# Products in different row halves of the array issued in turn, and a tap table stored contiguously, in a two-layer RWKV-7 / S5 trunk

## Chip, core and metric

The kernel runs on one core of a Trainium2 chip. The core has TensorE (PE in the profile; its weight loads are PEld), VectorE (DVE), ScalarE (ACT), GpSimd (POOL), and SyncE (SP), whose queue issues all DMAs here. The metric is the device time of one execution in microseconds; lower is better. Matrix products write to PSUM; the kernel's four PSUM pools hold eight banks of 128 partitions x 512 float32.

## What is computed

A batch of one sequence, 1024 frames of 1024 channels, goes through two layers. Layer 0 mixes frames with RWKV-7 (16 heads of 64 channels, a 64x64 state per head); layer 1 with a diagonal complex state-space scan (64 groups of 16 channels with 64 states each). Each mixer is followed by a squared-ReLU MLP, and every sub-layer by a residual and a LayerNorm.

```python
def step(state, inp):                       # RWKV-7, per head
    r_t, w_t, k_t, v_t, a_t, b_t = inp
    sa = einsum('bhvk,bhk->bhv', state, a_t)
    state = state * w_t + sa[..., None] * b_t + v_t[..., None] * k_t
    return state, einsum('bhvk,bhk->bhv', state, r_t)
...
w_pre = w0 + tanh(xw @ w1) @ w2             # "rates": decay and in-context rate
a = sigmoid(a0 + (xa @ a1) @ a2)
...
s = abar * s + bbar @ u                     # S5, complex, per group
y = Re(c @ s) + d * u
x = layer_norm(alpha * x + f(x)); f = mixer or square(relu(x @ w1)) @ w2
```

## The kernel before

Channels lie on partitions and frames on the free axis, in two halves of 512 frames. The large products run as float32r triples: operand and weight are each split into a high and a low part (`split`, line 148/149), and `mm3` issues high x high, high x low and low x high. Weights are streamed as 256 KB blocks (`wload`: one DMA on SP, a cast on ACT, a subtraction on DVE). The other products are plain float32; the trace shows each of them as two weight loads and two matmuls, which are called **records** here (256 chunk products of line 596 are 512 records).

A product whose operands lie on 64 partitions uses one half of the array's rows; one with 64 weight columns uses one half of its columns. The trace shows this as rows*columns, for example 64*128.

The order of the work is that of a list scheduler: every instruction has a priority (the `rank` blocks), and the scheduler lays out each engine's queue when the kernel is built. On the chip every engine then runs its queue in that fixed order. The places that the change touches:

- **Rates** (`rates`, line 382, 16 calls in the projection stage). The second factors of decay and rate lie in the upper and lower 64 rows of one weight tile; six products of 64 rows x 512 frames go into two banks `pp[0]`, `pp[1]` of the three-bank pool `pd`.
- **Chunk matrices** (`amat`, line 580, for 8 units in the RWKV core). For each of two channel groups `j` and two chunk pairs `c2`, eight products of 64 rows (line 596) make four chunk matrices for head half `h` = 0 in one bank and four for `h` = 1 in another. Both are the tag "a" of pool `pa`, which has two banks; `elem` of the next unit uses the same two banks for its own small products. DVE masks each bank into `AT` (line 599). The masked matrices go into `invert` and into `chain`, the recurrence over chunks (pR, pX, pU, pO).
- **Tap table** (`s5_tables`, line 1038). For 8 blocks `f` of 128 channels the taps of the causal convolution within 8 frames are computed (line 1151), copied by ACT into the padded tile `kpad` with the group index innermost (line 1155), and stored by two DMAs for each `f` into `tT` (line 1159). The tables `tB` (input to state) and `tC` (state to output) are stored in the same loop.
- **Readout** (`s5`, from line 1235, once for each half of the frames). For four pairs `f2` of blocks, `tT` and `tC` are loaded into four buffers of the tag "tab". For each parity `par`, eight **tap products** (line 1250, all 128 rows, 64 columns, moving operand `tv` at a step of four elements) and sixteen **state products** (line 1255, the 64 rows that belong to `par`) are summed in one bank `py` of the two-bank pool `pc`. ACT copies each bank into `y1` (line 1257); eight transposes per block and a GELU follow, and the result goes out to `s_y`, which the GLU loads again. MLP products stand between the pairs `f2`.

## Time and profile before

| | |
|---|---|
| Median of three runs | 2736.43 us (2736.28 to 2744.62) |
| Profiled execution, its own time | 2746.6 us |
| Span of its trace | 2744.8 us |
| Mean granted TensorE clock | 0.961 |
| DVE / ACT / POOL busy | 66% / 42% / 23% |
| DMA | 345.90 MB, 126 GB/s on the mean |

Durations below come from the profiled execution, so sums are made against 2746.6 us and then carried over to the median. A matmul is pipelined: its duration is longer than the distance to the next one's start, so the cost of a run of matmuls is read from the start of its first to the start of what follows it. In a timeline row the first number is the start in us, the second the time from the first start to the last end, and x is the number of records. In a row of the groups, the numbers after the bar are busy us, mean ns of one, and idle us before them.

### The profile page before, as it was taken

To read this page: it belongs to the slowest core of one execution; us is meant where nothing else is said; L and a number is where in the kernel's file an instruction comes from. 1 tells how busy PE (TensorE), PEld (TensorE's weight loads), DVE (VectorE), ACT (ScalarE), POOL (GpSimd) and SP (SyncE) were. 2 spreads that over 40 slices of the span, in tenths; PEclk is the share of its full clock that TensorE was granted. 3 is DMA by queue.
4 is the path that set the end of the run, shared out by engine and by line. 5 is a ranking of instruction groups with operands and counts; after the bars stand their busy time and mean duration, and the time that the engine had idled before them with its cause. 6 is when DMAs were issued, how large, how long until landed. Compare 5 with 4: busy or idle time off the path is not lost.

```text
span 2744.8 us, 43807 instructions
## 1 busy us (share of the span) xinstructions
PE 2598.4 (95%) x16582; PEld 2089.9 (76%) x16582; DVE 1813.3 (66%) x3191; ACT 1154.8 (42%) x2038; POOL 630.6 (23%) x515
## 2 busy tenths in 40 slices
PE   7999979989899999989999999999999999999997
PEld 5778757678677777767876788778778887788886
DVE  7477677577786867997567553674855546755556
ACT  7455574544543333353532332434223324433334
POOL 3121542432442122342122000120220101210101
PEclk9989979999899999999999999999999999999998
DMA  4765455564223334545333533233343322333333
GB/s 146 235 214 175 151 164 156 178 203 142 81 86 88 93 92 148 141 129 163 100 112 127 174 95 100 81 96 112 103 164 110 96 96 81 119 96 96 96 96 100
DMA packets 215058, 345.90 MB, mean 126 GB/s; under 512 B 21184, under 2 KB 75584, under 8 KB 214848
## 3 DMA queue, kind: packets, MB, share of 16 engines
q1 hardware_dynamic: 214848, 343.10, 40.5%
q8 instruction: 131, 2.15, 0.3%
q14 instruction: 79, 0.65, 0.1%
HBM read 279.06 MB, written 63.96 MB: 125 GB/s over the span
## 4 chain that ended last, share of the span: by engine, by line
PE 44%; DVE 4%; issue 3%; DMA 1%; POOL 1%; ACT 1%; ACTq 0%; SPq 0%; DVEq 0%; POOLq 0%
PE d L188 39%; PE py L1250 1%; PE py L1255 1%; DVE wlo L149 1%; DMA wraw<-in_mw_dram 1%; PE pu L154 1%; PE pbu L1206 1%; POOL rl L975 1%; DVE hA L991 0%; DMA s_y<-yg 0%; DVE t L1218 0%; DVE hB L991 0%; ACT whi L148 0%; DVE sq L876 0%; PE pu L1195 0%
## 5 line engine op out<-in xcount | busy, mean ns | idle before, releaser
L148 ACT CAST whi<-wraw 128x512 fp32r<-128x512 f32 x668 | 413.5, 620 | 929.1 <-PE d L188 623.2
L149 DVE TENSOR_TENSOR wlo<-wraw,whi 128x512 fp32r<-128x512 f32 x668 | 500.6, 750 | 426.8 <-ACT whi L148 404.3
L188 PE MATMUL d<-qbuf,whi 128*128 128x512 f32 (+1 forms) x2112 | 657.0, 394 | 23.8 <-DVE hA L991 12.8
L188 PEld LDWEIGHTS d<-qbuf,whi 128*128 128x128 f32 x2112 | 391.8, 191 | 120.0 <-DVE hA L991 17.8
L188 PE MATMUL d<-qbuf,wlo 128*128 128x512 f32 (+1 forms) x1056 | 411.9, 392 | 10.7 <-DVE wlo L149 10.4
L975 POOL TENSOR_TENSOR rl<-rl 128x512 f32<-128x512 f32 x128 | 157.2, 1228 | 1094.5 <-ACT rl L974 1094.5
L188 PE MATMUL d<-oAh,whi 128*128 128x512 f32 (+1 forms) x960 | 390.9, 411 | 15.5 <-ACT ev L418 6.3
L188 PE MATMUL d<-oAl,whi 128*128 128x512 f32 (+1 forms) x960 | 387.5, 405 | 3.0 <-DVE oAl L149 2.8
L188 PE MATMUL d<-oAh,wlo 128*128 128x512 f32 (+1 forms) x960 | 386.5, 405 | 2.4 <-DVE wlo L149 2.3
L188 PE MATMUL d<-oBh,whi 128*128 128x512 f32 x704 | 279.2, 397 | 0.0
L188 PE MATMUL d<-oBh,wlo 128*128 128x512 f32 x704 | 278.7, 396 | 0.2 <-DVE wlo L149 0.2
L188 PE MATMUL d<-oBl,whi 128*128 128x512 f32 x704 | 277.1, 394 | 0.0
L188 PEld LDWEIGHTS d<-qbuf,wlo 128*128 128x128 f32 x1056 | 201.7, 191 | 56.5 <-DVE wlo L149 14.5
L188 PEld LDWEIGHTS d<-oAh,whi 128*128 128x128 f32 (+1 forms) x960 | 185.9, 194 | 62.2 <-ACT ev L418 8.4
L188 PEld LDWEIGHTS d<-oAh,wlo 128*128 128x128 f32 (+1 forms) x960 | 185.8, 194 | 44.4 <-DVE wlo L149 3.2
L188 PEld LDWEIGHTS d<-oAl,whi 128*128 128x128 f32 (+1 forms) x960 | 185.6, 194 | 43.1 <-DVE oAl L149 5.2
L991 DVE TENSOR_TENSOR hB<-hB,d 128x512 f32<-128x512 f32 (+1 forms) x256 | 165.0, 650 | 71.2 <-PE d L188 68.0
L991 DVE TENSOR_TENSOR hA<-hA,d 128x512 f32<-128x512 f32 x240 | 162.1, 682 | 64.4 <-PE d L188 62.1
L188 PEld LDWEIGHTS d<-oBh,wlo 128*128 128x128 f32 x704 | 132.9, 189 | 32.4 <-issue 2.0
L188 PEld LDWEIGHTS d<-oBl,whi 128*128 128x128 f32 x704 | 133.1, 189 | 29.9 <-issue 0.7
L188 PEld LDWEIGHTS d<-oBh,whi 128*128 128x128 f32 x704 | 133.1, 189 | 29.0 <-issue 1.2
L149 DVE TENSOR_TENSOR qbuf<-rl,qbuf 128x512 fp32r<-128x512 f32 x128 | 95.0, 742 | 73.5 <-ACT qbuf L148 73.5
(374 smaller groups left out, 3804.8 us busy)
## 6 DMA issues: line engine op xcount, KB each, us to landing
wraw<-in_mw_dram SPq DMA_DIRECT2D x520, 256.0 KB, 2.7
wraw<-in_glu_dram SPq DMA_DIRECT2D x64, 256.0 KB, 2.7
low<-wlo SPq DMA_DIRECT2D x52, 256.0 KB, 2.6
wlo<-low SPq DMA_DIRECT2D x52, 256.0 KB, 3.6
wraw<-in_wk_dram SPq DMA_DIRECT2D x32, 256.0 KB, 3.5
wraw<-in_wr_dram SPq DMA_DIRECT2D x32, 256.0 KB, 3.9
wraw<-in_wv_dram SPq DMA_DIRECT2D x32, 256.0 KB, 4.3
yl<-s_y SPq DMA_DIRECT2D x32, 256.0 KB, 3.1
```

Source lines behind the costliest of these rows:

```text
L148: S.copy(hi, src)
L149: (e or V).tensor_sub(lo, src, hi.bitcast(F32))
L154: PE.matmul(out, x, idt, start=True, stop=True)
L188: bulk.append((PE.matmul(p, w, x, **kw).ins, x.shape[-1]))
L975: G.tensor_mul(r, r, r)
L991: V.tensor_add(z, z, p)
L1206: PE.matmul(p[qs, g2, ri], tb[:, g2, ri, qs], u[:, 2 * g2 + par], start=True, stop=True)
L1250: PE.matmul(p[64 * j : 64 * j + 64, g2], ug[f][:, 2 * g2 + par], tv[:, par, g2], start=g2 == 0, stop=False, skip_group_check=True)
L1255: PE.matmul(p[64 * j : 64 * j + 64, g2], hb[qs, 4 * f + g2, ri, 0:NSC], tcm[qs, g2, ri], start=False, stop=ri == 1, skip_group_check=True)
```

## The change

Nothing that is computed changes. Four things do:

1. A helper `inorder` ties products together so that the scheduler keeps them in the order in which they are written. `mmb` now returns its matmul.
2. Rates and chunk matrices are written with the two row halves in turn (half 1 first), each into its own bank, and tied.
3. In the readout both parities' banks are opened together: sixteen tap products first, with the parities in turn, then 32 tied state products that go around (column half j, row half par). The two copies to `y1` stand behind all of them.
4. `kpad` is four times as large (four blocks `f`), with the taps of a group contiguous, and is stored after every fourth block by 2 x 8 DMAs of 16 partitions x 16 pieces of 128 elements. `tT` is laid out by partition; a load takes two pieces of 512 elements for each partition, and the tap products read a contiguous moving operand.

```diff
+TBF = 4
+    def inorder(prods):
+        for x, y in zip(prods, prods[1:]):
+            tc.add_manual_dep(y.ins, x.ins.name, ... NoSync ..., reason="order")
...
             for wi, xi in ((0, 0), (0, 1), (1, 0)):
-                for j in range(2):
+                for j in (1, 0):
                     js = slice(64 * j, 64 * j + 64)
-                    mmb(pp[j], w2[0][n % 4][wi][js], hx[xi][js], ...)
+                    prods.append(mmb(pp[j], w2[0][n % 4][wi][js], hx[xi][js], ...))
+            inorder(prods)
...
                     for i in range(2):
-                        for h in range(2):
+                        for h in (1, 0):
-                            PE.matmul(pp[h][:, cc, i], D.KB[j][hs, u], D.AR[j][hs, u], ...)
+                            prods.append(PE.matmul(pp[h][:, cc, i], D.KB[j][hs, u], D.AR[j][hs, u], ...))
+                inorder(prods)
...
-    tT = dr.tile([KT, 128, 2, 512], F32, name="tT")
+    tT = dr.tile([128, 2, KT, 4, 128], F32, name="tT")
-        kpad = pp.tile([128, 16, 16, 4], F32, name="kpad")
+        kpad = pp.tile([128, TBF, 4, 16, 16], F32, name="kpad")
...
-                S.copy(kpad[ps_, 8:].rearrange("p t c g -> p g (t c)"), p[ps_])
-            for par in range(2):
-                src = kpad[64 * par : 64 * par + 16, 1:9].rearrange("p t c g -> p (t c g)")
-                SP.dma_start(tv[par], bass.AP(src.tensor, src.offset, [src.ap[0], (64, SL), src.ap[1]]))
+                S.copy(kpad[ps_, f % TBF, :, 8:].rearrange("p g t c -> p g (t c)"), p[ps_])
+            if f % TBF == TBF - 1:
+                for par in range(2):
+                    for s in range(SL):
+                        SP.dma_start(
+                            tT[16 * s : 16 * s + 16, par, f - TBF + 1 : f + 1].rearrange("c f g n -> c (f g) n"),
+                            kpad[64 * par : 64 * par + 16, :, :, 1 + s : 9 + s].rearrange("c f g t e -> c (f g) (t e)"))
...
-            for par in range(2):
-                for g2 in range(4):
-                    for j, (f, tv, tcm) in enumerate(tabs):
-                        PE.matmul(p[64 * j : 64 * j + 64, g2], ug[f][:, 2 * g2 + par], tv[:, par, g2], ...)
-                for g2 in range(4):
-                    for ri in range(2):
-                        for j, (f, tv, tcm) in enumerate(tabs):
-                            PE.matmul(p[64 * j : 64 * j + 64, g2], hb[qs, 4 * f + g2, ri, 0:NSC], tcm[qs, g2, ri], ...)
-                S.copy(y1[:, :, :, par], p)
+            for g2 in range(4):
+                for par in range(2):
+                    for j, (f, tv, tcm) in enumerate(tabs):
+                        PE.matmul(pp[par][64 * j : 64 * j + 64, g2], ug[f][:, 2 * g2 + par], tv[:, par, g2], ...)
+            prods = []
+            for g2 in range(4):
+                for ri in range(2):
+                    for j, (f, tv, tcm) in enumerate(tabs):
+                        for par in range(2):
+                            prods.append(PE.matmul(pp[par][64 * j : 64 * j + 64, g2],
+                                                   hb[qs, 4 * f + g2, ri, 0:NSC], tcm[qs, g2, ri], ...))
+            inorder(prods)
+            for par in range(2):
+                S.copy(y1[:, :, :, par], pp[par])
```

**PE, chunk matrices of one unit of the core, before.** The number behind pA names the bank's tile; neighbouring tiles are the two row halves of one pair. Rows with d are projection products.

```order
L596 MATMUL pA_3972<-AR_3728,KB_3729 128x128 x4
L596 MATMUL pA_3983<-AR_3794,KB_3795 128x128 x4
L188 MATMUL d_4872<-oAl_4861,whi_4917 128x512
L188 MATMUL d_4872<-oAh_4860,wlo_4918 128x512
L188 MATMUL d_4871<-oAl_4868,whi_4911 128x512
L188 MATMUL d_4871<-oAh_4867,wlo_4912 128x512
L188 MATMUL d_4872<-oAh_4867,whi_4917 128x512
L708 MATMUL pX_3917<-o_3851,XT_3513 64x64 x8
L188 MATMUL d_4872<-oAl_4868,whi_4917 128x512
L188 MATMUL d_4872<-oAh_4867,wlo_4918 128x512
L596 MATMUL pA_3984<-AR_3794,KB_3795 128x128 x4
L596 MATMUL pA_3995<-AR_3794,KB_3795 128x128 x4
```

The same unit after the change, its first pair (pb and pn are small products of `elem`, pv1 belongs to `invert`):

```order
L555 MATMUL pn_3778<-ident_84,sq_3764 128x128 x4
L584 MATMUL pb_3804<-rksel_105,kf_3790 64x1
L608 MATMUL pA_3960<-AR_3728,KB_3729 128x128
L584 MATMUL pb_3804<-rksel_105,kf_3790 64x1 x15
L608 MATMUL pA_3959<-AR_3728,KB_3729 128x128
L608 MATMUL pA_3960<-AR_3728,KB_3729 128x128
L608 MATMUL pA_3959<-AR_3728,KB_3729 128x128
L608 MATMUL pA_3960<-AR_3728,KB_3729 128x128
L608 MATMUL pA_3959<-AR_3728,KB_3729 128x128
L608 MATMUL pA_3960<-AR_3728,KB_3729 128x128
L608 MATMUL pA_3959<-AR_3728,KB_3729 128x128
L665 MATMUL pv1_3585<-x1_3511,AT_3320 32x32 x32
```

Before, four products of one half stood together, often directly ahead of four of the other half of the next pair. Now the first product stands alone where its bank comes free, and the other seven follow, halves in turn, where the second bank is free. Over the program 11 of the 32 pairs stand in one piece and 21 are cut behind the first product or later.

**PE, readout of one pair f2, before** (py is the bank, tt and tcm are the tables of the two blocks, 13973 and 13977 the two column halves):

```order
L1250 MATMUL py_13979<-tt_13971,ug_13550 64x128
L1250 MATMUL py_13979<-tt_13975,ug_13581 64x128
L1255 MATMUL py_13979<-tcm_13973,hb_13435 64x128
L1255 MATMUL py_13979<-tcm_13977,hb_13435 64x128
L1255 MATMUL py_13979<-tcm_13973,hb_13435 64x128
```

And after:

```order
L1266 MATMUL py_13996<-tt_13987,ug_13566 64x128
L1266 MATMUL py_13996<-tt_13991,ug_13597 64x128
L1274 MATMUL py_13995<-tcm_13989,hb_13451 64x128
L1274 MATMUL py_13996<-tcm_13989,hb_13451 64x128
L1274 MATMUL py_13995<-tcm_13993,hb_13451 64x128
L1274 MATMUL py_13996<-tcm_13993,hb_13451 64x128
```

The state products went around two quarters of the array (one row half, two column halves); now they go around all four, in two banks. What stands around the readout on PE is the same as before, and the same in number.

**SP, storing of the tables, before** (two of the eight blocks f):

```order
L1159 DMA tT<-kpad 16x8x512 x2
L169 DMA wraw<-in_mw_dram 128x512
L1110 DMA bc<-in_s5bc_dram 128x256
L169 DMA wraw<-in_mw_dram 128x512
L1168 DMA tB<-bs 128x1024
L1144 DMA tC<-ca 1024x1x128
L169 DMA wraw<-in_mw_dram 128x512
L1159 DMA tT<-kpad 16x8x512 x2
```

And after, at the fourth block:

```order
L170 DMA wraw<-in_wo_dram 128x512
L1172 DMA tT<-kpad 16x16x128 x16
L1183 DMA tB<-bs 128x1024
L1157 DMA tC<-ca 1024x1x128
L1123 DMA bc<-in_s5bc_dram 128x256
L170 DMA wraw<-in_wo_dram 128x512
L170 DMA wraw<-in_mw_dram 128x512
```

Two DMAs at each block became sixteen in a row at the fourth and the eighth, ahead of the other tables' stores, the next block's inputs and the next weights. On ACT the copy into `kpad` for the fifth block now waits for those sixteen DMAs.

More of the change, by code (lines that the diff above doesn't have):

```diff
@@ new lines, in s5 @@
+                tabs.append((f, tt.rearrange("p two (g n) -> p two g n", g=4), tcm))
+            pp = [r.tile([128, HT], F32, tag=t, name="py").rearrange("p (g n) -> p g n", g=4)
+                  for r, t in ((pc, "c"), (pc, "c"))]
+            for g2 in range(4):
+                for par in range(2):
+                    for j, (f, tv, tcm) in enumerate(tabs):
+                        PE.matmul(pp[par][64 * j : 64 * j + 64, g2], ug[f][:, 2 * g2 + par], tv[:, par, g2],
+                                  start=g2 == 0, stop=False, skip_group_check=True)
@@ L1258, in s5 @@
+            inorder(prods)
+            for par in range(2):
+                S.copy(y1[:, :, :, par].rearrange("p t g c -> p g t c"), pp[par].rearrange("p g (t c) -> p g t c", t=SL))
             for j in range(2):
```

28 lines of the change are left out of this document (14 added, 14 removed).

## Prediction

> **What bounds the kernel.** I read the page's engine shares and its chain first, then a table of stretches, then the rows of the products that the change touches.
>
> ```profile
> PE 2598.4 (95%) x16582; PEld 2089.9 (76%) x16582; DVE 1813.3 (66%) x3191; ACT 1154.8 (42%) x2038; POOL 630.6 (23%) x515
> PE 44%; DVE 4%; issue 3%; DMA 1%; POOL 1%; ACT 1%; ACTq 0%; SPq 0%; DVEq 0%; POOLq 0%
> ```
>
> TensorE is busy for 95% of the span, and it is by far the largest engine in the chain that ended last. So time taken from TensorE can shorten the kernel, but not everywhere alike:
>
> ```profile
> core 0: us, PE busy (x) PEld busy (x) DVE busy (x) ACT busy (x) POOL busy (x), PEclk, DMA share, GB/s
> 0.00:1110.00 1110.00, 1021.50 (x8345) 825.14 (x8346) 791.03 (x1589) 561.08 (x1033) 341.81 (x288) 0.93 0.47 147
> 1110.00:1270.00 160.00, 143.31 (x785) 108.69 (x784) 150.66 (x245) 68.13 (x104) 65.84 (x46) 0.94 0.53 141
> 1390.00:1535.00 145.00, 137.35 (x921) 104.36 (x920) 97.90 (x154) 43.51 (x73) 34.64 (x18) 0.98 0.43 142
> 1535.00:1925.00 390.00, 388.41 (x1952) 316.23 (x1950) 219.67 (x328) 148.15 (x253) 51.99 (x47) 1.00 0.33 100
> ```
>
> RWKV layer (to 1110): TensorE busy 1021.50 of 1110, 92%. Table stage (1110 to 1270): DVE busy 150.66 of 160, so DVE bounds it. Readout of the first half (around 1390 to 1535) and all that follows: TensorE busy 95 and then nearly 100%. In the readouts a microsecond saved on TensorE should be nearly a microsecond of the kernel; in the RWKV layer, a part of one; in the table stage, nothing.
>
> **The tap and state products (readout).** A piece of the timeline, with tap products at line 1250 and state products at line 1255:
>
> ```profile
> 1489.60 1.01 PE L1263 MATMUL pyt<-ident,y 64*128 64x64 f32 x16
> 1490.55 2.01 PE L1250 MATMUL py<-tt,ug 128*64 128x128 f32 x14
> 1492.49 1.96 PE L1255 MATMUL py<-tcm,hb 64*64 64x128 f32 x32
> 1494.38 2.01 PE L1250 MATMUL py<-tt,ug 128*64 128x128 f32 x16
> 1496.33 1.96 PE L1255 MATMUL py<-tcm,hb 64*64 64x128 f32 x32
> 1498.22 0.51 PE L188 MATMUL d<-oBh,whi 128*128 128x512 f32 x1
> ...
> 1399.47 2.08 PE L1206 MATMUL pbu<-ug,tb 128*64 128x64 f32 x64
> 1401.39 1.07 PE L1250 MATMUL py<-tt,ug 128*64 128x128 f32 x4
> ```
>
> Start to start, 16 tap records take 1496.33 - 1494.38 = 1.95 us, 0.122 each; 32 state records take 1498.22 - 1496.33 = 1.89 us, 0.059 each. Both stream 128 elements and alternate the two column halves. They differ in rows (128 against 64) and in the step of the moving operand (4 against 1). The rows are not the cause: line 1206, with 128 rows, a step of 1 and half the width, takes (1401.39 - 1399.47)/64 = 0.030, which is 0.060 at this width. So a contiguous tap table brings 256 records from 0.122 to 0.059: 256 x 0.063 = **16 us**, and a little at the heads of runs. Bounds: 0, if neither comparison carries over, and 256 x 0.092 = 24, if records came at line 1206's 0.030 whatever their width; I take 17.
>
> For the state products I expect the two row halves to run side by side, as the column halves do already. Two row halves in two banks with all columns are shown by the chunk matrices:
>
> ```profile
> 131.06 1.16 PE L596 MATMUL pA<-AR,KB 64*128 64x128 f32 x8
> 132.15 0.50 PE L188 MATMUL d<-oAl,whi 128*128 128x512 f32 x1
> ...
> 429.62 1.71 PE L596 MATMUL pA<-AR,KB 64*128 64x128 f32 x16
> 431.26 0.50 PE L188 MATMUL d<-oAh,whi 128*128 128x512 f32 x1
> ...
> 914.95 1.17 PE L596 MATMUL pA<-AR,KB 64*128 64x128 f32 x16
> 916.05 0.55 PE L609 MATMUL pT<-ident,KB 128*128 128x128 f32 x3
> ...
> 551.18 0.48 PE L596 MATMUL pA<-AR,KB 64*128 64x128 f32 x2
> 551.60 0.69 PE L713 MATMUL pU<-vsa,kbt 128*64 128x64 f32 x16
> ```
>
> Eight records of one half alone take 1.09 us (131.06 to 132.15). At 914.95 the scheduler happened to mix the halves, and 16 records take 1.10. At 429.62 one half stands wholly ahead of the other, and 16 take 1.64. Mixed halves thus cost half. All four quarters at once appear nowhere in this trace. If they work, 512 state records go from 0.059 to 0.030: 15 us; if not, 0. I take **14**, since both kinds of overlap are shown singly.
>
> Each pair f2 also gets later copies: both banks are copied after all products, two ACT copies in a row. Behind them the order has some 21 dense products (5.0 us, below) ahead of the transposes that need `y1`, and these cover the copies; without them it would be about 1.2 us for each of 8 pairs, two copies at about the span of one 512-element ACT copy, 0.6. The next tables are loaded when their four buffers are released:
>
> ```profile
> 1498.29 5.04 PE d L188 x21
> ...
> DMA to landing us min/median/max: 4.3/5.4/7.0
> ```
>
> The first row is a piece of the chain, 21 dense products; the second the landing of `tcm` in the first half's readout. After the change its first use follows the last release by those 21 products (5.0), 16 transposes (0.9 to the next start) and 30 tap records (1.8), 7.7 us; an issue like line 1159's below (0.36) and the landing take 5.8, at worst 7.4. It just fits, and I cost it at 0; an overrun costs under 2 us in each of six rounds.
>
> **Chunk matrices.**
>
> ```profile
> L596 PE MATMUL pA<-AR,KB 64*128 64x128 f32 x512 | 65.4, 295 | 3.1 <-DVE AT L599 2.4 <-DVE kk L545 0.7
> L599 DVE TENSOR_TENSOR AT<-pA,amask x64: 661/683/693, 127.6 to 929.2; 128x512 f32<-128x512 f32 x64
> ```
>
> Busy 65.4 us now. After the change 11 pairs stand in one piece, at 1.17 each (914.95): 12.9. The other 21 begin with one product alone, 0.48 (551.18), and seven more take 7/8 of 1.17 and a head, about 1.06: 21 x 1.54 = 32.3. Together 45.2, a saving of **20 us**; bounds 0 and 65.4 - 32 x 1.17 = 28. The change adds a wait: on PE the second bank's first product now holds up six products and then dense ones or the hops of the recurrence, until DVE has masked (0.68 us) the bank before.
>
> **Rates.**
>
> ```profile
> 55.51 0.75 PE L188 MATMUL d<-stash,whi 64*128 64x512 f32 x4
> 56.08 0.41 PE L188 MATMUL d<-stash,wlo 64*128 64x512 f32 x2
> ...
> 70.84 0.73 PE L188 MATMUL d<-stash,whi 64*128 64x512 f32 x2
> 71.41 0.39 PE L188 MATMUL d<-stash,wlo 64*128 64x512 f32 x1
> 71.73 0.50 PE L188 MATMUL d<-oAh,wlo 128*128 128x512 f32 x1
> ```
>
> At 55.51 the scheduler had put three products of one half ahead of three of the other; still the six were over after about 0.98 us, no longer than three products alone at 70.84 (0.89 to the next). Halves that stand side by side in a short run overlap already. Only about five of the 16 calls were apart by more than that: 5 x 0.9 = 4.5, less a little for calls that are now cut after their first product. I take **4** (0 to 8).
>
> Here the Trainium skill says more for the change. "TensorE: Matmul & The Clock Gate", section Packing small matmuls, says that matmuls start and end strictly in program order, tiles of the array included. By that the six at 55.51 would have taken about 1.4 us; all 16 calls would gain, 9 us rather than 4, and the kernel would come out near 2686 rather than at my forecast. The row speaks against it.
>
> **Tables and queues.**
>
> ```profile
> L1155 ACT COPY kpad<-pk x16: 1055/1074/1087, 1126.9 to 1267.7; 16x512 f32<-16x512 f32 x16
> L1159 SPq DMA_DIRECT2D tT<-kpad x16: 320/362/1264, 1128.6 to 1268.9; - x16
> DMA to landing us min/median/max: 3.9/4.7/5.8
> ...
> 1170.43 2.17 ACT L1155 COPY kpad<-pk 16x512 f32<-16x512 f32 x2 [2.41 <-PE pk L1151]
> ...
> 1189.61 2.15 ACT L1155 COPY kpad<-pk 16x512 f32<-16x512 f32 x2
> ```
>
> Sixteen ACT copies become contiguous, some 0.5 us shorter each; ACT has 68 of 160 us busy there, so this is worth nothing. The memset of `kpad` is four times as large, on a POOL that is 41% busy: nothing. Sixteen DMAs in a row hold SP for 16 x 0.36 = 5.8 us and land 4.7 to 5.8 later: 11 to 12 us. Behind them stand a store of each other table, the next inputs and weights. On ACT the fifth block's copy waits for all sixteen, with the weight casts behind it, and dense products behind those. Between the fourth copy's end (1172.6) and the fifth's start (1189.6) lie 17 us, so I cost it at 0; if the small pieces land slower, 0 to 6.
>
> **Sum.** Readout 17 + 14 = 31, all realised, as TensorE bounds these stretches and what follows. RWKV layer 20 + 4 = 24, of which I count 14: TensorE is 92% busy there, which is nearer to all than to nothing, but its idle time is waits on DVE, ACT and loads that do not shrink, and the new wait is one more. Tables 0. Together 45 us: 2746.6 - 45 = 2701.6 for an execution like the profiled one. That execution lies 10 us above the median, so for the median 2736.4 - 45 = **2691**.
>
> **Rivals.**
>
> *The quarters do not add up* (15%). Products of four quarters share one supply of weights or moving data and keep 0.059 for a record. For it: each state record waits for a weight load of its own, and no row shows four. Against: overlap is shown by rows and by columns. Price: 14 us; 2705.
>
> *The bank pair eats the gain of the RWKV layer* (17%). Both banks of a pair now fill together, but DVE empties them one by one, 2 x 0.683 = 1.37 us against 1.10 of products. "TensorEngine Tiling (Array Packing)", section PSUM Bottleneck, in the Trainium skill, warns of this: tiling speeds up the products but not the evacuation. For it: the pool has two banks only, and `elem` needs them as well. Against: only 3.1 us of waits stand in the row of line 596. Price: the whole 14 us; 2705. With both rivals (3%) 2719.
>
> *Slower than before* (6%). The bank taken by the first product of a cut pair stands idle until the second is free, and `elem` of the next unit, which feeds the next hops, waits for one of the same two. It becomes slower when each of 32 pairs puts more than 45/32 = 1.4 us on the path of the recurrence, about the two masks of a pair one after the other. At 2.4 us the kernel would stand near 2768. The pairs have TensorE work of other tiles between them, so I hold it for unlikely.
>
> *It does nothing visible* (6%). The tied order could change little because products overlap already, as at 55.51, and the scheduler's other order in the RWKV layer could cost what the readout gains. The tap table's 17 us would still be there; with 10 to 17 lost elsewhere, near 2732.
>
> **Range and chances.** The forecast holds 53%. Its own range is 2674 (56 us of TensorE time all realised, and a few us of heads) to 2700. The range that should hold 8 in 10 reaches to the two single rivals and their joint case: 2674 to 2719. Runs of this kernel can tell 0.3%, 8 us, from no change. Faster by more than that: forecast, first two rivals and their joint case, 0.88, less 0.02 for a joint case with a late table stage: 0.86. Within it: 0.08. Slower: 0.06.
>
> **What would show it.** Tap records at 0.06 a piece and two-record means near 270 ns; state records at 0.03; line 608 with about 45 us busy; 16 records of a pair near 1.1 us; no long idle time in front of the fifth copy to `kpad`; the RWKV layer ending some 14 us earlier and each readout 15 us shorter. The forecast is wrong if state records stay at 0.059, if waits on `AT` masks in front of line 608 grow to tens of us, or if tables land after their readers.

## The result, and the profile after

The changed kernel is slower: 2765.77 us (median of 4 runs, 2763.88 to 2767.27) against 2738.43 us (4 runs of the kernel before, 2736.28 to 2744.62) beside it, a ratio of 1.0096 with a 95% interval of 1.0083 to 1.0109. The prediction had said 2691 us. The profiled execution took 2765.87 us, its span is 2764.0. The profiled execution of the kernel before took 2746.6 us, 8 us above its median; so tables of the two traces show less of the loss than the medians do, and their single rows can be off by some us.

The engine shares and the chain that ended last, on the page of the changed kernel:

```profile
PE 2553.0 (92%) x16582; PEld 2054.6 (74%) x16582; DVE 1810.2 (65%) x3191; ACT 1147.9 (42%) x2038; POOL 626.9 (23%) x515
PE 50%; DVE 11%; DMA 5%; issue 3%; ACT 2%; SPq 2%; POOL 1%; ACTq 0%; DVEq 0%; POOLq 0%
```

TensorE is busy 2553.0 us instead of 2598.4, so its work did become 45 us shorter. The span grew by 19.2 us all the same; TensorE's idle time grew by 45.4 + 19.2 = 65 us. In the chain that ended last, DVE has 11% instead of 4, DMA transfers 5% instead of 1, and SP's queue 2% instead of 0. Where the time went, shows a table of stretches, cut at events that both kernels have: the first copy to `kpad`, the first `pu` of each readout half, the last GELU of `yg` of each (`pu` is the transposed input of the S5 scan, with which its work on a half begins; `yg` is y). First the kernel before, then the changed one; after the length come busy us and records of PE and its weight loads, then the other engines, granted clock and DMA share.

```profile
0.00:1126.90 1126.90, 1038.40 (x8442) 838.27 (x8442) 807.89 (x1639) 564.70 (x1039) 346.49 (x292) 0.93 0.47 146
1126.90:1327.40 200.50, 182.95 (x943) 141.21 (x944) 176.39 (x259) 88.06 (x138) 74.53 (x53) 0.95 0.52 142
1327.40:1541.80 214.40, 206.75 (x1452) 160.99 (x1451) 130.20 (x203) 74.72 (x127) 38.81 (x22) 0.98 0.42 136
1541.80:1858.60 316.80, 315.25 (x1390) 256.52 (x1389) 185.60 (x277) 116.35 (x200) 47.80 (x43) 1.00 0.32 95
1858.60:2070.60 212.00, 204.64 (x1446) 160.04 (x1445) 128.85 (x200) 72.38 (x125) 37.55 (x22) 0.98 0.39 128
2070.60:2744.80 674.20, 650.47 (x2919) 532.89 (x2917) 384.34 (x618) 238.63 (x415) 85.44 (x83) 0.98 0.33 98
```

```profile
0.00:1101.20 1101.20, 996.55 (x8356) 800.26 (x8356) 786.89 (x1612) 561.28 (x1031) 346.48 (x292) 0.94 0.47 148
1101.20:1352.50 251.30, 206.29 (x1032) 157.65 (x1033) 187.21 (x290) 86.97 (x148) 74.22 (x53) 0.90 0.45 121
1352.50:1561.80 209.30, 190.50 (x1441) 151.58 (x1439) 131.13 (x199) 71.80 (x124) 35.65 (x22) 0.97 0.43 139
1561.80:1880.90 319.10, 317.69 (x1392) 258.72 (x1393) 186.50 (x278) 116.99 (x200) 47.86 (x43) 0.99 0.30 94
1880.90:2089.60 208.70, 191.18 (x1442) 152.41 (x1440) 131.18 (x199) 71.40 (x125) 37.77 (x22) 0.96 0.40 129
2089.60:2764.00 674.40, 650.75 (x2922) 534.02 (x2922) 387.24 (x619) 239.41 (x415) 84.88 (x83) 0.99 0.32 99
```

Three things stand in it.

- **RWKV layer and tables, up to the first `pu`** (two rows each): 1327.4 us became 1352.5. The first row, 26 us shorter, is not all gain: 86 records fewer stand ahead of the first `kpad` copy and 89 more behind it, dense products that the scheduler moved. Busy fell by 18.5 us over both rows, idle time rose from 106 to 150.
- **The two readouts** (rows 3 and 5): busy 411.4 us became 381.7, 30 less, but the time only 426.4 to 418.0, 8 less. Idle time rose from 15 to 36 us. Of both figures some 3 us are no gain: 15 records fewer stand in these rows, dense products at 0.229 us each from start to start.
- The other two rows are 2.5 us longer together; they hold 9 of these dense products more (dense: line 188, 195 after the change).

The products themselves did what the prediction said. A piece of the timeline and the groups of the changed kernel:

```profile
1512.04 1.96 PE L1266 MATMUL py<-tt,ug 128*64 128x128 f32 x30
1513.93 1.98 PE L1274 MATMUL py<-tcm,hb 64*64 64x128 f32 x64
1515.84 0.50 PE L195 MATMUL d<-oBh,whi 128*128 128x512 f32 x1
...
L608 PE MATMUL pA<-AR,KB 64*128 64x128 f32 x512 | 56.9, 318 | 13.6 <-DVE AT L612 8.5 <-DVE kk L556 2.7 <-DVE bo L586 2.0
L1266 PE MATMUL py<-tt,ug 128*64 128x128 f32 x256 | 22.8, 311 | 10.3 <-DMA tt<-tT 10.3
L1274 PE MATMUL py<-tcm,hb 64*64 64x128 f32 x512 | 16.9, 284 | 0.0
```

Tap records take 1.89/30 = 0.063 us from start to start (0.122 before), state records 1.91/64 = 0.030 (0.059 before): half the time for each, for the taps with a contiguous operand, for the state products with all four quarters of the array in turn. What is new is on the right: 10.3 us of waits for `tt`, and 8.5 us in front of the chunk matrices where 2.4 had stood.

The table stage around the first burst of stores: SP's queue (the second number is the time from the first issue to the end of the last), and TensorE in four stretches of 10 us, two at each burst. Then who waited, in total us, times and longest: two rows of the changed kernel from 1100 to 1300 us, and one of the kernel before, from 1110 to 1300.

```profile
1155.01 18.92 SPq L1172 DMA_DIRECT2D tT<-kpad  x16
1174.03 1.29 SPq L1183 DMA_DIRECT2D tB<-bs  x1
1175.41 1.34 SPq L1157 DMA_DIRECT2D tC<-ca  x1
1176.84 1.60 SPq L1123 DMA_DIRECT2D bc<-in_s5bc_dram  x1
1178.50 1.10 SPq L170 DMA_DIRECT2D wraw<-in_wo_dram  x1
...
1253.91 19.34 SPq L1172 DMA_DIRECT2D tT<-kpad  x16
...
L1172 SPq DMA_DIRECT2D tT<-kpad x32: 326/1288/1859, 1155.0 to 1271.7; - x32
...
1170.00:1180.00 10.00, 2.73 (x10) 1.31 (x9) 0.78 (x2) 0.82 (x2) 0.00 (x0) 0.69 0.85 172
1180.00:1190.00 10.00, 4.21 (x13) 2.40 (x12) 8.09 (x12) 2.07 (x4) 5.26 (x4) 0.50 0.37 126
1260.00:1270.00 10.00, 2.20 (x10) 1.47 (x8) 1.37 (x2) 0.21 (x1) 0.00 (x0) 0.80 0.75 101
1270.00:1280.00 10.00, 0.00 (x0) 0.00 (x0) 0.11 (x1) 0.00 (x0) 0.00 (x0) 0.50 0.79 162
...
ACT whi L149 <- DMA wraw<-in_mw_dram: 50.3, 11, 19.9
PE d L195 <- ACT whi L149: 21.8, 3, 18.6
...
ACT whi L148 <- DMA wraw<-in_mw_dram: 27.4, 11, 3.9
```

One store in the burst takes 0.33 us to issue at best, but 1.29 in the median. The sixteen hold SP for 19 us, the next inputs and weights (`bc`, `wraw`) stand behind them, and then TensorE is busy for 9 of 40 us, at a granted clock of 0.50 to 0.80. DVE, ACT and POOL stand nearly still too, in three of the four stretches. At the first burst TensorE waits 7.2 us for ACT's second copy into `kpad` for the fifth block, which starts at 1178.55 only, 23.5 us after the first store was issued; at the second it waits 18.6 us for a weight.

### The profile page after: what moved, and what is told of

It reads as the page before. It is cut to its first block, busy times and chain, and to the rows that moved or that the text cites. A ratio compares the mean times of both kernels' runs of the same rounds, so it can differ in the third digit from the quotient of the medians.

```text
span 2764.0 us, 43770 instructions
## 1 busy us (share of the span) xinstructions
PE 2553.0 (92%) x16582; PEld 2054.6 (74%) x16582; DVE 1810.2 (65%) x3191; ACT 1147.9 (42%) x2038; POOL 626.9 (23%) x515
## 4 chain that ended last, share of the span: by engine, by line
PE 50%; DVE 11%; DMA 5%; issue 3%; ACT 2%; SPq 2%; POOL 1%; ACTq 0%; DVEq 0%; POOLq 0%
PE d L195 46%; DVE wlo L150 2%; DMA wraw<-in_mw_dram 2%; SPq L1172 1%; DMA s_y<-yg 1%; DMA yl<-s_y 1%; DVE hA L1004 1%; PE pbu L1221 1%; PE pu L155 1%; ACT whi L149 1%; POOL rl L988 0%; DVE qbuf L150 0%; DVE sq L889 0%; DVE t L1233 0%; DVE hB L1004 0%
## 5 line engine op out<-in xcount | busy, mean ns | idle before, releaser
L195 PE MATMUL d<-oAh,whi 128*128 128x512 f32 (+1 forms) x960 | 391.7, 411 | 35.8 <-ACT whi L149 18.8
L988 POOL TENSOR_TENSOR rl<-rl 128x512 f32<-128x512 f32 x128 | 152.4, 1190 | 1090.3 <-ACT rl L987 1082.0
```

What stands on the lines that cost most here:

```text
L195: r = PE.matmul(p, w, x, **kw)
L988: G.tensor_mul(r, r, r)
```

## Experiments

Each ratio is to the kernel before, run on the same chip at the same time, with its 95% interval.

### The orders alone, and the table alone

The first kernel keeps rates, chunk matrices and state products of the change, with the tap table of before; the second is its complement.

```diff
 e1_orders: the changed kernel, with the table of before
-tT = dr.tile([128, 2, KT, 4, 128], F32, name="tT")
+tT = dr.tile([KT, 128, 2, 512], F32, name="tT")
...
 e2_table: the kernel before, with the table of the change
+            if f % TBF == TBF - 1:
+                for par in range(2):
+                    for s in range(SL):
+                        SP.dma_start(tT[16 * s : 16 * s + 16, par, f - TBF + 1 : f + 1]..., kpad[...])
```

> The change without its table part: the orders of rates, chunk matrices and state products as in the changed kernel, the tap table, its stores and its loads as before. Theory A (the two bursts of sixteen stores hold SP, and the weights behind them come late: the changed kernel goes from 21 us ahead at 1047 us to 25 us behind at the first pu, 46 us): no loss in the table stage, so the 19 us of the RWKV layer stay, and the state products add 5 to 15: 2703 to 2716 us. Rival B (the earlier end of the RWKV layer moves DVE and weight work into the table stage, and the loss comes whatever the stores are): 2738 us or more.

> The kernel before with the table part alone: contiguous tap table, sixteen stores after the fourth and the eighth block. Theory A: the table stage loses some 46 us and the taps give back up to 17: 2765 to 2785 us, with two stretches of 15 us or more in which TensorE is nearly idle, at the two bursts. Rival B: the bursts alone cost little, and the taps gain: 2722 to 2738 us.

The orders alone: 2740.13 us, ratio 1.0007 (0.9995 to 1.0019). No loss, but no gain either: theory A was right about the slowdown and missed on the time. Rival B's range holds the time, but not its reason: without the bursts TensorE is busy for 19.3 of 20 us from 1170 to 1190 in this trace, and 17.8 of 20 from 1260 to 1280, and the first `pu` starts at 1329.2, as in the kernel before (1327.4). The copy into `kpad` starts 18.5 us earlier than before, about as much as the 86 dense products take that moved behind it, so it is no gain of the RWKV layer. The table alone: 2756.85 us, 1.0068 (1.0043 to 1.0094), between theory and rival; both bursts are there again, 18.9 and 20.3 us long. The loss belongs to the table.

### What makes the burst slow

```diff
 e3_tbf1: sixteen stores of 32 KB after each block
-TBF = 4
+TBF = 1
...
 e4_alternate: the two groups of partitions in turn
-                for par in range(2):
-                    for s in range(SL):
+                for s in range(SL):
+                    for par in range(2):
...
 e12_pool: issued from POOL's queue
-                        SP.dma_start(
+                        G.dma_start(
...
 e14_wide and e16_wide2: the same 128 KB in 256 pieces of 512 bytes, read from 128 partitions
-  tT[16 * s : 16 * s + 16, par, ...], kpad[64 * par : 64 * par + 16, :, :, 1 + s : 9 + s]...
+  tT[:, par, ...]..., kpad[:, 2 * par : 2 * par + 2]...[:, :, 128 * s : 128 * s + 128]      (e14)
+  tT[:, par, ...]..., kpad[:, 2:4, s % 4, 8:16]...                                          (e16)
```

> The changed kernel with TBF = 1: the sixteen stores follow each block, 32 KB each and of the same 512-byte pieces, so as many bytes and packets in eight small bursts of 512 KB. Theory A (a burst holds SP for its bytes at some 105 GB/s): 5 us for each block, spread over 160 us, covered as before: first pu some 40 us earlier than in the changed kernel, 2720 to 2732 us. Rival C (pieces of 512 bytes are slow to store and the sum of the stores counts, not their bunching): 2760 us or more. Rival D (128 DMAs cost SP 128 x 0.33 = 42 us of issue and hold the weights as much): 2745 us or more.

> The changed kernel with the two loops of the sixteen stores exchanged: the same DMAs, those that read partitions 0 to 15 and those that read 64 to 79 in turn, instead of eight and eight. Theory E (the rate of 105 GB/s is that of the few partitions that are read; the Trainium skill's page SBUF - State Buffer, section on the DMA port swizzle, puts partitions 0 to 15 and 64 to 79 on different ports, and would let the two groups move side by side): sixteen stores hold SP for 10 to 12 us instead of 19, about 16 us less over both bursts and some wait at TensorE with it: 2735 to 2752 us. Rival C (the limit is the write, the pieces or one queue): 2763 to 2768 us, and 19 us a burst.

Small bursts after each block gained nothing: 2765.45 us, 1.0105 (1.0088 to 1.0121), as rivals C and D had it; e16_wide2 below, with pieces of the same size, speaks against C. Its 128 DMAs hold SP some 7.4 us for each block, and the weights and `bc` come late as before; the second row is TensorE in the worst 20 us.

```profile
1175.04 7.35 SPq L1172 DMA_DIRECT2D tT<-kpad  x16
...
1180.00:1200.00 20.00, 6.14 (x51) 4.24 (x50) 9.33 (x14) 3.46 (x6) 4.62 (x5) 0.78 0.53 149
```

The groups in turn gained 10 to 13 us over the changed kernel (by the ratios and by the medians): 2753.07 us, 1.0058 (1.0038 to 1.0077), 1 us above the range of theory E. The DMAs are the same; a burst became shorter, 12.6 us:

```profile
1155.82 12.60 SPq L1172 DMA_DIRECT2D tT<-kpad  x16
```

That the two groups would move side by side was the expectation's own inference from their lying on different ports; the rate rose by half, it did not double.

> The changed kernel with its 32 stores of the tap table issued from POOL's queue instead of SP's; order, sizes and bunching as in the changed kernel. Theory S (the cost is that SP is held 19 us in each burst, with weights and the next inputs behind): the first pu comes 15 to 23 us earlier than in the changed kernel, 2742 to 2752 us. Rival Q (the transfers themselves slow the weights' transfers on the shared DMA engines, or POOL held back costs the tables as much): 2758 us or more.

> The changed kernel, with each of the 32 stores of the tap table reading 128 partitions instead of 16: the same number of DMAs, the same 128 KB and 256 pieces of 512 bytes each, bunched in the same places (the table is filled with other numbers, so the output is not the reference's). Theory E (the burst is slow because each store reads few partitions): pieces of 512 bytes take about 27 ns as elsewhere instead of 61 to 65, a burst holds SP 8 to 11 us instead of 19, 2738 to 2750 us. Rival C (the pieces, the bunching or the writes are slow): 19 us a burst and 2763 us or more.

> As e14_wide, mended: there most stores needed only an early part of the padded table, and so ran spread over the stage, not in a burst. Now each of the 32 stores reads 128 partitions and what the last block of its burst wrote, so that all sixteen wait for the fourth and the eighth block as in the changed kernel (the table is filled with other numbers, so the output is not the reference's). Theory E (few partitions read make the burst slow): 512-byte pieces near 27 ns, a burst over in 8 to 11 us, 2734 to 2748 us. Rival R (e14_wide gained because its stores were spread, not because they were wide): bursts of 15 us or more, 2755 us or more.

Issuing from POOL did not help: 2768.13 us, 1.0099 (1.0077 to 1.0122). SP holds none of the stores there, and yet weights come late: three loads issued during the burst took 2.2 to 5.3 us to issue instead of 0.33, and then long to land. Landing times of `wraw`, first from 1060 to 1140 us (22 loads), then from 1165 to 1195, around the first burst (four loads, one of them issued before it):

```profile
DMA to landing us min/median/max: 2.4/2.7/6.2
...
DMA to landing us min/median/max: 2.6/12.5/18.8
```

So theory S fell: not SP's queue alone is what is short; a burst from POOL's queue slows SP's loads as well. The Trainium skill, "DMA: Bandwidth & Descriptors", section Issuing engines are not separate DMA queues, says that DMAs of all queues run on the same 16 engines; this run agrees, and the time is in rival Q's range. What POOL's own delay cost (0.56 us of issue for each store) is not told apart.

The wide stores of e14_wide (2734.05 us, 0.9979, 0.9966 to 0.9992) came below the range of theory E and did not answer the question alone: many of them needed little of `kpad` and ran ahead of the burst. In e16_wide2 all sixteen stand together again: 2738.57 us, 0.9996 (0.9986 to 1.0007), 27 us less than the changed kernel and as theory E had it, with a burst of

```profile
1159.11 8.37 SPq L1172 DMA_DIRECT2D tT<-kpad  x16
```

Three bursts of the same 16 x 128 KB = 2.10 MB thus took 18.9 us from one group of 16 partitions at a time (111 GB/s), 12.6 from two groups in turn (166 GB/s), and 8.4 from 128 partitions (250 GB/s, at 0.52 us of issue for each DMA). The packets of 512 bytes in these stretches (1157 to 1177, 1157 to 1171 and 1160 to 1170 us) took 60, 40 and 29 ns in the mean of the trace's records. That the partitions read set the length of the burst is shown, by three sizes of it; the second has the very same DMAs as the first, in another order. The third changes more: its pieces go to other places in DRAM, and its stores read nothing that the fifth block's copy writes, so that ACT need not wait for them. That copy started at 1172.24 there, behind a wait for TensorE, when the burst was over; so little of the 27 us can be due to it.

The Trainium skill has the rule: "SBUF — State Buffer", section Door 1: The DMA port swizzle, says that DMA bandwidth depends on how many of 16 ports the partitions reach, that partitions 0 to 15 reach 4 of them, and gives about 109 GB/s for these. The 111 GB/s here agree.

### Why the readout gave back most of its 30 us

On SP the changed kernel issues, after the products that ended at 1515.84:

```profile
1513.92 0.33 SPq L1289 DMA_DIRECT2D s_y<-yg  x1
1514.30 0.53 SPq L1255 DMA_DIRECT2D tt<-tT  x1
1514.93 0.57 SPq L1257 DMA_DIRECT2D tcm<-tC  x1
1516.06 0.32 SPq L959 DMA_DIRECT2D yl<-s_y  x1
1518.07 0.32 SPq L1289 DMA_DIRECT2D s_y<-yg  x1
1518.49 0.53 SPq L1255 DMA_DIRECT2D tt<-tT  x1
1519.11 0.57 SPq L1257 DMA_DIRECT2D tcm<-tC  x1
...
1523.94 1.96 PE L1266 MATMUL py<-tt,ug 128*64 128x128 f32 x30 [1.47 <-DMA tt<-tT]
```

The second `tt` was read for the last time at 1513.93, when the tap products were over. Its load is issued at 1518.49, because the store of the second y of the pair before stands ahead of it in SP's queue, and that y waits for the first one's store (there is one `yg` buffer). So the taps wait at 1523.94. Of the 21 us by which idle time grew in the readouts, such waits for `tt` are 10.3; transposes that wait for ACT's copies of y are 5.4 (none before), and dense products waiting for DVE's `hA` and `hB` 12.7 instead of 8.0.

The trace of e1_orders bears this out: its taps are as long as before (36.6 us busy), they wait 4.9 us for `tt` instead of 10.3, and both readouts take 418 us, as in the changed kernel. So on top of the shorter state products the shorter taps brought nothing. In four traces with the readout of before (before, e7_chunk, e8_before_early, e13_less) the two take 423 to 427 us.

More kernels test the chain:

```diff
 e5_tge: orders of the change; two stores for each block as before, rows in the order t, group, c
 (its lines against the kernel before)
-kpad = pp.tile([128, 16, 16, 4], F32, name="kpad")
+kpad = pp.tile([128, 16, 4, 16], F32, name="kpad")
-tt.rearrange("p two (n g) -> p two g n", g=4)
+tt.rearrange("p two (t g c) -> p two g t c", g=4, c=16)
...
 e6_early: e5_tge, with the loads of the next pair written behind the products of a pair
+            if f2 < 3:
+                nxt = tables(f2 + 1)      # both tt first, then both tcm
             for par in range(2):
                 S.copy(y1[:, :, :, par]..., pp[par]...)
...
 e9_yg2: e6_early, with two y buffers (e10_before_yg2: the same line in the kernel before)
-y = s5p.tile([128, HT], F32, tag="yg", name="yg", bufs=1)
+y = tp.tile([128, HT], F32, tag="la", name="yg", bufs=2)
```

e8_before_early has the early loads in the kernel before.

> Rates, chunk matrices and state products ordered as in the changed kernel, but the tap table stored once per block by two DMAs of 2048-byte rows as before, with each row in the order t, group, c (before: t, c, group): the tap products then read runs of 16 contiguous elements, and nothing is bunched. Measured so far: the orders alone (old table) 2740 us. Theory F (in the readout TensorE is no longer the bound once its products are shorter: the next tables' loads stand behind the stores of y in SP's queue, which wait for the y chain): tap records fall to about 0.06 us, but the time stays within 4 us of the orders alone, 2736 to 2743 us. Rival G (TensorE bounds the readout as the prediction said, and only the bursts spoilt it): 17 us less than the orders alone, 2720 to 2727 us. Rival K (runs of 16 are no better than a step of 4): tap records stay near 0.12 us, time 2740 us.

> The kernel e5_tge, with the loads of the next pair's tables written right behind the products of a pair, both tap tables first: on SP they then stand ahead of the second store of y of that pair instead of behind it. Nothing else changes. Theory F: the waits of tap products for tt (about 6 us in the first half's readout and 4 in the second's in the changed kernel) go, 5 to 12 us less than e5_tge, 2726 to 2736 us. Rival G: no wait of that kind binds, same as e5_tge within 3 us. Rival M (behind the loads the y chain itself, one yg buffer and the round trip through s_y, is the bound): tt waits go, but the time stays within 3 us of e5_tge.

> The kernel before with the early loads of e6_early alone (control): before has no wait for tables in its readouts, so all theories expect no change, 2735 to 2743 us; if it is faster by as much as e6_early is over e5_tge, the early loads help for another reason than the one named.

> The kernel e6_early with two buffers for y behind Gelu instead of one (taken from the two 2 KB buffers that the layer norms use as la, so no memory is added). In e6_early the second y of a pair waits 2.8 to 3.3 us for the store of the first to land (1484.19, 1498.97), its store is issued 4.5 to 5 us after the first, the two tcm loads stand behind that store, and state products wait 8.9 us for tcm in both readouts. Theory M (this chain bounds the readout of the changed kernel): those waits go, 6 to 14 us less than e6_early, 2720 to 2728 us. Rival N (behind it the readout is bound by the dense products' own inputs or by loads, or the layer norms now wait for la): within 3 us of e6_early, 2731 to 2737 us.

> The kernel before with two buffers for y alone (control). Theory M: TensorE bounds the readout of before (its rounds of 14.3 us a pair hide the chain), so no change: 2736 to 2744 us. If it gains as much as e9_yg2 does over e6_early, the gain does not come from the shorter products having uncovered the chain.

e5_tge: 2736.8 us, 0.9988 (0.9972 to 1.0004). Its taps are as short as in the changed kernel (22.9 us busy), nothing is bunched, and the time still is that of before: as theory F said, and not G. e6_early: 2734.04 us, 0.9977 (0.9963 to 0.9992). The early loads alone in the kernel before: 2738.49 us, 0.9997 (0.9982 to 1.0013), no change, as expected. The groups of e5_tge and e6_early show what happened:

```profile
L1264 PE MATMUL py<-tt,ug 128*64 128x128 f32 x256 | 22.9, 312 | 8.5 <-DMA tt<-tT 8.5
```

```profile
L1277 PE MATMUL py<-tcm,hb 64*64 64x128 f32 x512 | 19.5, 293 | 8.9 <-DMA tcm<-tC 8.9
L1269 PE MATMUL py<-tt,ug 128*64 128x128 f32 x256 | 17.8, 277 | 0.7 <-DMA tt<-tT 0.7
```

The waits for `tt` went, from 8.5 us to 0.7, and 8.9 us of waits for `tcm` took their place, the next loads in the queue. The gain of 2.8 us between the two medians is smaller than their spread, and is what rival M said; that the wait moved is shown, that the time follows it is not.

Two y buffers on top: 2734.56 us, 0.9977 (0.9958 to 0.9997), theory M missed, and the time is as rival N had it. Both readouts together became shorter, 404.7 us against 418.0 in the changed kernel, but they also hold 29 records fewer (29 x 0.229 = 6.6 us of dense products, which stand behind them now), so about half of the 13 us is a gain, and state products still wait 8.4 us for `tcm`.

```profile
1320.90:1524.00 203.10, 184.81 (x1429) 146.84 (x1427) 129.25 (x195) 71.21 (x123) 35.70 (x22) 0.98 0.43 140
1846.40:2048.00 201.60, 185.53 (x1425) 148.21 (x1424) 129.37 (x195) 71.06 (x124) 38.22 (x22) 0.97 0.40 131
```

The same buffer in the kernel before: 2736.81 us, 0.9985 (0.9969 to 1.0001), which can't be told from no change.

### Why the RWKV layer gained nothing

```diff
 e7_chunk: the kernel before, with the chunk matrices in the order of the change
 e11_banks: e9_yg2, with a pair's banks from two pools
-pp = [pa.tile([128, 2, 2, 128], F32, tag="a", name="pA") for h in range(2)]
+pp = [r.tile([128, 2, 2, 128], F32, tag=t, name="pA") for r, t in ((pa, "a"), (pc, "c"))]
...
 e13_less: the kernel before; in squares(), second half of the frames
-                        mm3(pp[j], *ws[j][k], *xm[k0 + k], k0 + k == 0, k0 + k == KT - 1)
+                        mmb(pp[j], ws[j][k][0], xm[k0 + k][0], start=k0 + k == 0, stop=False)
+                        mmb(pp[j], ws[j][k][0], xm[k0 + k][1], start=False, stop=k0 + k == KT - 1)
```

e15_nochunk is e9_yg2 with the chunk matrices as before, e17_readout is e15_nochunk with the rates as before too.

> The kernel before with the order of the chunk matrices alone changed. Theory H (the bank pair eats it: TensorE saves 9 to 13 us at pA, but waits for masks and other engines grow by as much): within 4 us of before, 2735 to 2743 us, with more idle time ahead of pA behind DVE's AT. Rival (the RWKV layer is bound by TensorE at 92%, as the prediction counted): 9 to 14 us faster, 2725 to 2731 us.

> The kernel e9_yg2 with the two banks of a chunk-matrix pair taken from two pools (one of pa's two and one of pc's two) instead of both of pa's, so that the next pair finds a bank free in each pool. Theory H2 (the pair waits because both of its banks are the two that DVE has still to empty): the wait of pA for AT (7.5 to 8.5 us on PE, 10 to 11 on the weight loads) falls below 3, and 4 to 10 us are gained over e9_yg2. Rival P (what bounds the RWKV layer is the recurrence, of which the masks are one step, and pc's banks are those of its hops): within 3 us of e9_yg2 or slower.

> The kernel before, with 128 dense products of the RWKV layer left out: those of the weights' low parts for k and r of the second half of the tokens (the result is a little less precise). 128 x 0.229 = 29 us of TensorE work of the kind that fills the waits of the recurrence. Theory P (the RWKV layer follows the recurrence and other engines; TensorE time that is saved there becomes idle time, whatever product it is saved at): up to 10 us less than before, 2730 to 2740 us. Rival H (TensorE bounds the layer, as its 92% suggest, and the chunk matrices gained nothing only because of the masks that their pairs now wait for): 18 to 29 us less, 2711 to 2722 us.

> The kernel e9_yg2 (all orders of the change, table in rows of t, group, c, early loads, two y buffers) with the chunk matrices in the order of before. Theory P: their order is worth nothing here, so within 4 us of e9_yg2 on either side, 2729 to 2738 us. Rival H: 5 us slower or more where the order of the chunk matrices gains something, 5 us faster or more where their masks cost.

> The kernel e15_nochunk with the rates too in the order of before: what is left of the change is in the readout (state products, table in rows of t, group, c, early loads, two y buffers). By theory P the RWKV layer's orders give nothing: within 4 us of e15_nochunk, 2728 to 2737 us. If the rates' 4 us of TensorE time count in the layer, 2 to 4 us slower.

The chunk matrices alone: 2739.49 us, 1.0002 (0.9989 to 1.0015), nothing. The group of e7_chunk, then of e11_banks:

```profile
L603 PE MATMUL pA<-AR,KB 64*128 64x128 f32 x512 | 61.3, 332 | 10.8 <-DVE AT L607 7.6 <-DVE bo L581 2.7 <-DVE kk L551 0.4
```

```profile
L608 PE MATMUL pA<-AR,KB 64*128 64x128 f32 x512 | 40.8, 291 | 5.7 <-DVE AT L612 4.6 <-ACT o L739 0.7 <-DVE gt L792 0.2
```

In e7_chunk 4 us less is busy than in the kernel before (65.4), and 7.7 us more stand idle in front (10.8 against 3.1), most of them for the mask of the bank before. In e11_banks a pair finds its banks more often: 40.8 us busy instead of the 58.2 of e9_yg2, and 4.6 us for the masks instead of 7.5. Theory H2 had asked for less than 3 and for 4 to 10 us; the time is no better, 2737.7 us, 0.9991 (0.9976 to 1.0006), as rival P expected.

Leaving out 128 dense products gave 2727.04 us, 0.995 (0.9932 to 0.9969): 14.3 us for 29, between theory and rival. To the first `pu` the trace shows 1308.6 us instead of 1327.4, 18.8 less for 35 us less of TensorE (1186.2 against 1221.4). So the layer gives back about half of what TensorE saves there, at dense products at least.

e15_nochunk: 2732.66 us, 0.9967 (0.995 to 0.9985), though its chunk matrices keep TensorE busy for 76.9 us, 18.7 more than in e9_yg2. e17_readout: 2737.05 us, 0.9977 (0.9963 to 0.9991). Neither order can be told from nothing in this layer.

By their intervals e6_early, e9_yg2, e15_nochunk and e17_readout are faster than the kernel before by 0.2 to 0.3%, e9_yg2 only just. e15_nochunk has the lowest ratio of those that compute the reference in full; the intervals of the four overlap.

## Why the prediction was wrong, by its own steps

- **Tap and state products, 17 + 14 us of TensorE**: right. 0.063 and 0.030 us a record, busy 40.4 to 22.8 and 32.5 to 16.9 us. The rival that the quarters do not add up is out.
- **Chunk matrices, 45.2 us busy**: mis-sized. 56.9, a saving of 8.5 us, not 20. A part of the pairs ran on a low clock: from 720 to 755 us, at a granted clock of 0.61, one in one piece took 2.08 us (at 732.98) where others take 1.16 (at 555.66). The prediction used the short time for all, while the 65.4 us of before hold slow pieces too (eight records in 2.07 instead of 1.16 us, at 199.57 and at 410.60). Seven products behind a lone first one took 1.16 us, not 1.06.
- **Rates, 4 us**: about right on TensorE, 22.6 to 18.9 us from start to start over all calls; the 9 us that would follow from strict program order were not seen. What it is worth in time, e15_nochunk and e17_readout can't tell.
- **"In the table stage, nothing"**, and **"Tables 0"**: the step that failed most. The text took 16 x 0.36 us of issue and a landing of 4.7 to 5.8 us for the last store, as if sixteen transfers landed side by side like two. The rows quoted there held the rate: two stores of 256 KB over in 4.7 us are 512 KB in 4.7, at most 112 GB/s, and by it sixteen of 128 KB take 19 us, which is what they took. That it fits so well is in part luck: those two stores read one group of partitions each, and their 4.7 us hold the wait for the landing. The bound of 6 us was for "small pieces"; pieces were not the cause, bytes from few partitions were. Measured price: the changed kernel is 27 us above e16_wide2.
- **"On ACT the fifth block's copy waits for all sixteen, with the weight casts behind it"**: the right wait, but 11 to 12 us were put against a cover of 17 where the trace shows 23.5: ACT's first copy of the fifth block waited 7.1 us for the stores, and its second started at 1178.55, another 9.2 us of waiting later (the view names the store of `tB`; the last of the sixteen, issued at 1172.4, would land at 1177.6 by the 5.2 us that these stores take in the median, an estimate). TensorE waited 7.2 us for it. For the loads of weights and inputs behind the stores no cover was worked out at all; at the second burst, where no such copy follows, TensorE waited 18.6 us for one weight.
- **Readout, "31, all realised"**: 8, and 5 without the products that moved out. TensorE was busy 95% there, but with products half as long the round of a pair met the next limit at once. "It just fits" was worked out from the release of the table buffers, without the store of y that stands ahead of the loads in SP's queue; this wait alone is 10.3 us at the taps. The later copies of y, said to be covered by dense products, cost 5.4 us of waits in front of the transposes. Even without the burst, and with both waits tried, 6 to 9 us below before is all that these versions reached.
- **RWKV layer, "of which I count 14"**: 0 measurable. Half of what TensorE saves does come through (e13_less), but the chunk matrices saved 4 us (e7_chunk) to 8.5 and paid 5 to 6 in waits for masks. That is the rival "the bank pair eats the gain", in size. In e11_banks fewer of these waits brought no time, so a second limit stands behind them; which one was not settled. The Trainium skill's warning ("TensorEngine Tiling (Array Packing)", section PSUM Bottleneck), that tiling speeds up the products but not the emptying of their banks, fits e7_chunk's row: 4 us less busy, 5.2 us more of waits for the masks.
- **"Slower than before" (6%)**: it came true by another mechanism than the one named. The chance stood on the bank pair alone; the burst, worked out at 11 to 12 us against a cover of 17, should have been the rival on that side.

The sum by measured terms: table +27, readout -8, RWKV layer 0 within a few us, the rest +2.5; 21 us, where the spans differ by 19.2 and the medians by 27. The 8 us between these two are the profiled execution of before, which lay that far above its median; which rows hold them the traces don't show. A slip in the range changes nothing: 17 + 14 + 24 are 55 us of TensorE time, not 56.

## What to carry to other kernels

Cost a group of transfers by its bytes and by the rate that the trace shows for such a source, not by one issue and one landing; here stores that read 16 partitions at a time were the slow ones, and loads beside them paid, whichever queue issued them. When a stretch is bound by an engine at 95%, work out how long the chains beside it take before counting a saving of more than the 5%: here SP's order and one y buffer stood right behind. A row that became shorter because work was moved out of it is no gain; compare the records in it too.

## What the runs showed of the hardware that was not expected

- The rate of a burst of stores by the partitions read: 111, 166 and 250 GB/s for 16, two times 16 in turn, and 128 partitions, with packets of 512 bytes at 60, 40 and 29 ns. At 250 GB/s SP's issue is nearly without a gap, and the DMA engines are 92% busy (1160 to 1170 us in e16_wide2); which of the two limits it there is not shown.
- Four loads issued around such a burst from another queue (e12_pool) landed in 12.5 us in the median and 18.8 at worst, where 2.7 is the median of 22 ahead of it.
- A moving operand in runs of 16 float32 is as fast as a contiguous one: 30 tap records in 1.89 us from 1514.11 to 1516.00 in e5_tge, 0.063 each, where a step of four elements took 0.122:

```profile
1514.11 1.96 PE L1264 MATMUL py<-tt,ug 128*64 128x128 f32 x30 [0.74 <-DMA tt<-tT]
1516.00 1.98 PE L1272 MATMUL py<-tcm,hb 64*64 64x128 f32 x64
```
